# Rotary turn of the dilated heads: on a contiguous copy in token order, with even and odd tokens taken apart in the score products

## The chip, the cores and the metric

The kernel runs on one core of a Trainium2 chip, in float32 throughout. The metric is the device time of one execution in microseconds (us); lower is better. The engines are named as the profile names them: PE (TensorE products), PEld (its weight loads), DVE (VectorE), ACT (ScalarE), POOL (GpSimd), SP (SyncE, here a queue of loads).

## What is computed

Two layers of a decoder trunk for 256 tokens of width 1024. Each layer has a mixer (gated linear attention, retention, and a softmax attention over dilated windows, merged by gates), a layer norm, a SwiGLU block and a second norm. The change lies in the dilated attention, which has three groups of four heads of 128 channels:

```python
for g, (window, dilation) in enumerate(((128, 1), (512, 4), (2048, 16))):
    qg = _rotary(dq[:, :, g], pos, 32, 5e5)     # first 32 channels turned by the token's angle
    kg = _rotary(dk[:, :, g], pos, 32, 5e5)
    o_g, lse_g = _dilated_window_attention(qg, kg, dv[:, :, g], window, dilation)
```

With `x1` and `x2` the first and second 16 of the 32 channels, the turn is `x1*cos - x2*sin` and `x2*cos + x1*sin`. In groups 1 and 2 a query sees only keys whose distance is a multiple of 4 or 16, so even tokens meet only even ones and odd only odd ones.

## The kernel before

All weights pass through PE as units of 128 x 1024, loaded by SP. Each unit is split into two float32r parts: the high part is a copy on ACT (sometimes DVE), the low part a subtraction on DVE (`make_hi`, `make_lo`). A product with the weights is three products of parts. `a_pair` makes 256 channels (two heads) for all 256 tokens with 48 products of 256 columns into a PSUM tile of the pool `pm` (three tiles); `b_group` makes 512 channels for 128 tokens with 24 products of 512 columns.

The order of each engine's instructions is fixed when the program is built. A main stream emits the products with the weights; after each step `tick` gives every side generator one turn (softmax, norms, the turn of the heads), and then emits the splits of the next unit. A planner keeps a rough clock for each engine (`issue`); a side generator calls `settle` and is not resumed until the planner believes that its operands have been there for 2400 ns (`MARGIN`). The engines then run their own rows strictly in that order and wait for each other by semaphores.

For each dilated group the main stream makes the values (in groups 1 and 2 by even and odd tokens: `chunk(2)` takes every second token of the stationary operand), then q and k, two pairs of heads each. After each pair it starts `dil_rot` (line 473), which moves the pair from PSUM to a block of SBUF and turns the first 32 channels. With the last k pair it starts `dil_group` (line 491): score products (line 518), maxima on DVE (line 521), exponentials on ACT (line 527), transposes, products with v, and in groups 1 and 2 a trip of the result through DRAM (`scr`, lines 566 and 571) that brings the tokens back in order.

Before the change `dil_rot` works like this: a shuffle on DVE swaps the two halves of 32 channels from PSUM into a scratch block; ACT copies the pair into the block; for groups 1 and 2 this copy writes even tokens first, so that neighbouring tokens are written 128 elements apart. Then DVE multiplies the swapped channels by the sine table, multiplies the 32 channels, read from PSUM again, by the cosine table into the block, and adds the two. The PSUM tile is given back after the second multiplication. The ACT copy and the shuffle read the same PSUM tile, and the program lets the copy wait for the shuffle.

A line that is a helper's stands for many places: DVE, ACT and POOL instructions show line 118, products line 130, transposes line 134, most DMAs line 138. Of names in the rows, `pm` is a PSUM tile of the main stream, `px` one of side work, `f` a block of the shared SBUF pools, `r` a float32r block (split weights, among others), `xh` and `xl` the two parts of the layer's input, `cst` the constants (turning tables, masks).

Of the kernel before, what the change touches and what calls it, by code (L numbers as in the profile page):

```python
# [54 lines left out]
def trunk(ctx: ExitStack, tc: tile.TileContext, wst, xt_in, x_in, cst, tri, pcol, wga, wa2, lnp, out):  # L55
# [7 lines left out]

    # ---- a rough clock in ns for each engine and tile: side work goes to the tensor engine when its operands
    # should be there, so that the products with the weights needn't wait behind it ----
    clk = {"P": 0.0, "A": 0.0, "V": 0.0, "G": 0.0, "D": 0.0}
# [7 lines left out]
    def when(log, ap, e):  # L74
        """When the last access in this log to any of the columns is over, as seen by engine e."""
        name, a, b = span(ap)
        return max([t + (e != "P" and OWN if by == e else HOP) for x, y, t, by in log.get(name, ()) if x < b and a < y], default=0.0)
# [62 lines left out]
    def settle(*aps, margin=MARGIN):  # L140
        """For a side generator: go on when these tiles should be there."""
        while any(when(written, a, "P") + margin > clk["P"] for a in aps):
            yield

# [1 line left out]
    class Blocks:  # L146
# [3 lines left out]
        def get(self, n=1):  # L150
            """For a side generator: the next n free blocks."""
            while len(self.free) < n:
                yield
            return [self.free.pop(0) for _ in range(n)]

        def main(self, n=1):
            """For the main stream."""
            left = 3000
            while len(self.free) < n:
                tick()  # L160
                left -= 1
                assert left, "blocks"
            return [self.free.pop(0) for _ in range(n)]
# [9 lines left out]

# [1 line left out]
    state = {"dma": 0, "made": 0, "whole": 0, "calm": False, "touched": 0, "freed": 0, "cap": NR // 2}  # L175
# [3 lines left out]
    def halves(u):  # L179
        """The first unit goes by halves, for an early start."""  # L180
        return (slice(0, 512), slice(512, 1024)) if u == 0 else (slice(0, 1024),)
# [61 lines left out]

# [1 line left out]
    side = []  # L245

    def spawn(g):
        side.append(g)

    def tick():  # L250
        for g in list(side):
            try:
                next(g)
            except StopIteration:
                side.remove(g)
        # the next unit: its first part when the engine is free for it, the second when the first should be there
        need = state["touched"] + 2
# [24 lines left out]

# [1 line left out]
    XH = T([128, KT, S], "xh", 1, F32R)  # L284
    XL = T([128, KT, S], "xl", 1, F32R)
    xts = [F2.main()[0] for _ in range(4)]

    # the input comes in five pieces of k-tiles: 0, 1, 2-3, 4-5, 6-7
    PIECES = ((0, 1), (1, 2), (2, 4), (4, 6), (6, 8))
# [13 lines left out]

    # products of zeros while the first loads are under way bring the tensor engine to its full clock
    zero = F2.main()[0]
# [15 lines left out]
    PC = T([128, L, 32], "pcol")  # L321
    # the turning tables fill 32 partitions of their columns; the gate's second matrix and its bias lie beside them
    WA2 = C[32:49, COLS["dilc"][0]:COLS["dils"][1]].rearrange("p (l c) -> p l c", l=L)
# [8 lines left out]
    def start_rest():  # L332
        """What the first products don't need."""
        dma(nc.scalar, C[0:32, 0:512], cst[0:32, 0:512], 32)
# [47 lines left out]

# [1 line left out]
    def tokens(v, tt, dl):  # L384
        """128 tokens: the tt-th half, or with dl = 2 those of remainder tt by 2."""
        return v[:, tt * 128:tt * 128 + 128] if dl == 1 else v.rearrange("p (i c) -> p c i", c=2)[:, tt, :]
# [11 lines left out]
    def b_group(units, lh, ll, tt, ps, dl=1, last=False):  # L398
        """ps [128 tokens, 512] from units of [2 k-tiles, 512 columns], a step for each unit."""
        n = len(units)  # L400
        for i, u in enumerate(units):
            b_unit(u, i, n, lh, ll, tt, ps, dl)
            if last:
                free(u)
            if i < n - 1:
                tick()

    def a_pair(units, rh, rl, ps):
        """ps [128 columns, 2, 256 tokens] from units of [4 k-tiles, 256 columns]."""
        n = len(units)  # L410
# [21 lines left out]

# [1 line left out]
    def ln_first(tt, c, ps, st):  # L434
# [36 lines left out]

# [1 line left out]
    def dil_rot(g, ps, dst):  # L473
        """Two heads' channels [128, 2, 256 tokens] into dst, their first 32 turned; dilated groups have even tokens first."""
        dl = 2 if g else 1
        (blk,) = yield from F2.get()
        t = blk[0:32, :]
        src = ps.rearrange("p (h i c) -> p h i c", h=2, c=dl)
        V.stream_shuffle(t, ps[0:32, :], SWAP)
        d4 = dst.rearrange("p (h c i) -> p h i c", h=2, c=dl)  # L480
        tr, to = t.rearrange("p (h i c) -> p h i c", h=2, c=dl), d4[0:32]
        act(d4, src, AF.Copy)
        def table(name):
            return cs(name)[0:32].rearrange("p (i c) -> p i c", c=dl).unsqueeze(1).to_broadcast([32, 2, S // dl, dl])
        V.tensor_mul(tr, tr, table("dils"))
        V.tensor_mul(to, src[0:32], table("dilc"))
        PM.put(ps)
        V.tensor_add(to, to, tr)
        F2.put(blk)

    def dil_group(l, g, dblk, m, den, outs):
        """Scores, softmax numerators and their products with v; outs gets [128 tokens, 512] for each tile."""
        qb, kb = dblk[g, 0], dblk[g, 1]
# [13 lines left out]
        for tt in range(2):  # L507
            nb = tt + 1 if whole else 1
            n = 128 * nb
            k0 = 0 if whole else tt * 128  # L510
            b = yield from PS.get(nb)
# [4 lines left out]
            for h in range(H):  # L516
                o = b[h // per][:, (h % per) * n:(h % per) * n + n]
                mm(o, qT[:, h, tt * 128:tt * 128 + 128], kT[:, h, k0:k0 + n], start=True, stop=True)
            for h in range(H):
# [91 lines left out]

# [1 line left out]
    def gla_gates(l, E):  # L613
# [147 lines left out]

# [1 line left out]
    def ret_all(l, pss, vb, sg):  # L763
# [102 lines left out]
    def head_out(l, key, o, col):  # L866
        """A branch's [tokens, heads] transposed, times its norm's gain when col is given, and split."""
        OH, OL = OT[l, key] = yield from R.get(2)
# [22 lines left out]

# [1 line left out]
    for l in range(L):  # L893
# [3 lines left out]

        # the projections for the branches: a step by tokens has two tiles, one by channels two pairs of heads
        douts = {}
# [26 lines left out]

        # the first two have their units in turns: either tile of tokens, or piece of the first input, gives them work
        us = take(8)
# [26 lines left out]
        for g in range(3):  # L955
# [3 lines left out]
            for which in range(2):  # L959
                for hp in range(2):  # L960
                    us = take(2)
                    ps = PM.main()[0]
                    a_pair(us, xh, xl, ps)
                    if hp == 0:
                        dblk[g, which] = F4.main()[0]
                    spawn(dil_rot(g, ps, dblk[g, which][:, hp * 512:hp * 512 + 512]))
                    if which and hp:
                        spawn(dil_group(l, g, dblk, m, den, douts))
                    tick()
# [20 lines left out]

        # merge gates and branch projections, by pairs of 128 columns
        state["cap"] = (NR - 10) // 2
# [39 lines left out]

        # output projection, then the first norm
        state["cap"] = (NR - 4) // 2
# [16 lines left out]

        # SwiGLU: the first 512 channels by tokens, the others by channels
        state["cap"] = (NR - 5) // 2
# [91 lines left out]
        for tt in range(2):  # L1145
            # of the last tile, the first half of the columns ends before the second begins
            st = T([128, 2, 6], "lnst", 2)
# [60 lines left out]
def _sums(np):  # L1208
    """Within each chunk of 64, a sixteenth of the sum up to a token and of the sum after it."""
    i = np.arange(128)  # L1210
# [5 lines left out]
def _stream(np, w_in, w_branch, w_out, w_gate, w_up, w_down):  # L1216
    """All weights in the order of use, as units of [128, 1024]."""
    w = np.empty((L * UNITS, 128, 1024), np.float32)
# [100 lines left out]
```

## Time and profile before

| | |
|---|---|
| median of 3 runs | 1068.72 us (1066.67 to 1068.91) |
| profiled execution: span from first to last instruction | 1066.5 us |
| mean granted TensorE clock | 0.995 of full |
| PE busy | 1049.8 us (98%), 7122 products |
| DVE busy | 706.6 us (66%) |
| ACT busy | 491.8 us (46%) |
| DMA | 192.25 MB, mean 180 GB/s |

The profile's times are those of one execution. Its span leaves out what lies before the first and after the last instruction; no other time of that execution is given, and the median of the runs stands 2.2 us above its span. Products on PE overlap, and their ends are modelled, so PE's busy share says little about how densely they follow each other; the distance between starts says it.

### The profile page before, as it was taken

How to read it: one execution, taken by the hardware profiler on the slowest of the kernel's cores; microseconds unless marked ns; L12 is line 12 of the kernel's file. 1: busy time of each engine (PE TensorE's matmuls, PEld its weight loads, DVE VectorE, ACT ScalarE, POOL GpSimd, SP SyncE). 2: the span in 40 equal slices, each digit the busy share in tenths (PEclk: the TensorE clock that was granted, in tenths of full speed). 3: DMA queues.
4: the chain of work that ended last, by engine and by line, in shares of the span. 5: the costliest groups of instructions: out<-in, count | busy, mean ns of one | idle time of the engine just before them, and what ended most of it. 6: DMA issues, size and time to landing. Idle time of an engine off the chain costs nothing.

```text
span 1066.5 us, 17475 instructions
## 1 busy us (share of the span) xinstructions
PE 1049.8 (98%) x7122; PEld 956.9 (90%) x7122; DVE 706.6 (66%) x1065; ACT 491.8 (46%) x734; POOL 17.9 (2%) x24
## 2 busy tenths in 40 slices
PE   9999999999999999999999998999999999999997
PEld 7998977799998899999889998877999988999996
DVE  6798755767658756554688777476676686556454
ACT  6475554444445444343364554553443445444330
POOL 0000000000000000000000000000000000000000
PEclk9999999999999999999999999999999999999999
DMA  8786633426656574555376355343375666655521
GB/s 325 248 267 194 197 109 111 158 80 225 190 172 223 168 287 164 194 191 200 121 268 220 124 173 183 92 136 122 118 220 185 186 209 232 223 197 167 194 94 40
DMA packets 55667, 192.25 MB, mean 180 GB/s; under 512 B 6258, under 2 KB 7410, under 8 KB 55587
## 3 DMA queue, kind: packets, MB, share of 16 engines
q1 hardware_dynamic: 50400, 180.38, 51.4%
q10 hardware_dynamic: 5186, 10.76, 3.0%
q8 instruction: 56, 0.92, 0.3%
q14 instruction: 25, 0.20, 0.1%
HBM read 187.93 MB, written 3.18 MB: 179 GB/s over the span
## 4 chain that ended last, share of the span: by engine, by line
PE 90%; DVE 4%; DMA 3%; ACT 1%; issue 1%; SPq 0%; ACTq 0%; DVEq 0%
PE pm L130 70%; PE px L130 18%; DVE f L118 2%; PE px L134 2%; DMA scr<-f 2%; DVE r L118 2%; ACT f L118 1%; DMA stage<-in_wst_dram 0%; DMA f<-scr 0%; ACT r L118 0%; DVE xres L118 0%; SPq L138 0%; ACTq L138 0%; DVE lnst L118 0%; DVEq L1314 0%
## 5 line engine op out<-in xcount | busy, mean ns | idle before, releaser
L130 PE MATMUL pm<-xh,r 128*128 128x256 f32 x2688 | 478.2, 280 | 0.0
L118 DVE SCALAR_TENSOR_TENSOR r<-stage,r 128x1024 fp32r<-128x1024 f32 (+1 forms) x341 | 401.7, 1213 | 59.4 <-ACT r L118 57.1
L130 PEld LDWEIGHTS pm<-xh,r 128*128 128x128 f32 x2688 | 413.1, 189 | 1.1
L118 ACT ACTIVATE r<-stage 128x1024 fp32r<-128x1024 f32 (+1 forms) x328 | 332.8, 1051 | 91.8 <-issue 31.3
L130 PE MATMUL pm<-xl,r 128*128 128x256 f32 x1344 | 374.9, 279 | 0.0
L130 PEld LDWEIGHTS pm<-xl,r 128*128 128x128 f32 x1344 | 252.4, 188 | 0.9
L130 PE MATMUL pm<-r,xh 128*128 128x512 f32 x672 | 218.4, 406 | 0.8 <-ACT r L118 0.8
L130 PEld LDWEIGHTS pm<-r,xh 128*128 128x128 f32 x672 | 124.8, 192 | 29.3 <-issue 3.0
L130 PE MATMUL pm<-r,xl 128*128 128x512 f32 x336 | 133.6, 398 | 0.0
L118 ACT ACTIVATE f<-pm 128x512 f32<-128x512 f32 x72 | 50.8, 707 | 156.6 <-PE pm L130 106.1
L130 PE MATMUL px<-r,r 128*128 128x512 f32 x528 | 122.6, 389 | 0.0
L130 PEld LDWEIGHTS px<-r,r 128*128 128x128 f32 x528 | 97.9, 188 | 19.3
L130 PE MATMUL pm<-r,r 128*128 128x256 f32 (+1 forms) x768 | 115.1, 310 | 0.0
L130 PEld LDWEIGHTS pm<-r,r 128*128 128x128 f32 x768 | 105.2, 191 | 7.3
L118 DVE SCALAR_TENSOR_TENSOR f<-f,pm 128x512 f32<-128x512 f32 x52 | 35.6, 685 | 106.6 <-ACT f L118 89.9
L130 PEld LDWEIGHTS pm<-r,xl 128*128 128x128 f32 x336 | 64.6, 192 | 14.3
L130 PE MATMUL px<-f,f 128*128 128x128 f32 (+4 forms) x368 | 60.4, 304 | 6.3 <-DVE f L118 6.3
L130 PEld LDWEIGHTS px<-f,f 128*128 128x128 f32 (+2 forms) x368 | 48.7, 185 | 16.7 <-issue 8.5
L118 ACT ACTIVATE r<-f 128x512 fp32r<-128x512 f32 x28 | 17.7, 632 | 98.9 <-DVE f L118 98.9
L118 ACT ACTIVATE f<-pm,hcol 128x256 f32<-128x256 f32 x48 | 20.1, 471 | 58.1 <-PE pm L130 58.1
L118 ACT ACTIVATE f<-px 128x512 f32<-128x512 f32 (+2 forms) x52 | 25.0, 507 | 42.6 <-PE px L130 29.4
L118 DVE TENSOR_TENSOR f<-f,pm 128x512 f32<-128x512 f32 x22 | 15.1, 687 | 41.0 <-PE pm L130 40.8
(102 smaller groups left out, 498.6 us busy)
## 6 DMA issues: line engine op xcount, KB each, us to landing
stage<-in_wst_dram SPq DMA_DIRECT2D x339, 512.0 KB, 4.5
f<-in_lnp_dram ACTq DMA_DIRECT2D x8, 512.0 KB, 6.3
scr<-f ACTq DMA_DIRECT2D x8, 260.0 KB, 4.8
f<-scr ACTq DMA_DIRECT2D x4, 520.0 KB, 3.6
xres<-in_x_dram ACTq DMA_DIRECT2D x4, 256.0 KB, 4.0
out_dram<-xres SPq DMA_DIRECT2D x4, 256.0 KB, 2.0
f<-in_xt_dram SPq DMA_DIRECT2D x3, 256.0 KB, 9.1
cst<-in_cst_dram ACTq DMA_DIRECT2D x4, 192.0 KB, 3.8
```

What stands on the lines that cost most here:

```text
L118: return f(*a, **k)
L130: return nc.tensor.matmul(out, lhsT, rhs, **k)
L134: return nc.tensor.transpose(out, in_, ident)
```

## The change

`dil_rot` no longer knows the group. ACT first copies the pair from PSUM into the block in token order, and the PSUM tile is given back. DVE then does everything on SBUF: shuffle from the block into the scratch, sine on the scratch, cosine in place on the block, sum, all in token order. The score products of groups 1 and 2 take the even or the odd tokens by reading every second column of q (the stationary operand) and of k (the moving operand).

```diff
-    def dil_rot(g, ps, dst):
+    def dil_rot(ps, dst):
-        dl = 2 if g else 1
         (blk,) = yield from F2.get()
-        t = blk[0:32, :]
-        src = ps.rearrange("p (h i c) -> p h i c", h=2, c=dl)
-        V.stream_shuffle(t, ps[0:32, :], SWAP)
-        d4 = dst.rearrange("p (h c i) -> p h i c", h=2, c=dl)
-        tr, to = t.rearrange("p (h i c) -> p h i c", h=2, c=dl), d4[0:32]
-        act(d4, src, AF.Copy)
-        def table(name):
-            return cs(name)[0:32].rearrange("p (i c) -> p i c", c=dl).unsqueeze(1).to_broadcast([32, 2, S // dl, dl])
-        V.tensor_mul(tr, tr, table("dils"))
-        V.tensor_mul(to, src[0:32], table("dilc"))
+        act(dst, ps, AF.Copy)
         PM.put(ps)
-        V.tensor_add(to, to, tr)
+        t, o = blk[0:32, :], dst[0:32, :]
+        V.stream_shuffle(t, o, SWAP)
+
+        def times(x, name):
+            x2 = x.rearrange("p (h t) -> p h t", h=2)
+            V.tensor_mul(x2, x2, cs(name)[0:32].unsqueeze(1).to_broadcast([32, 2, S]))
+        times(t, "dils")
+        times(o, "dilc")
+        V.tensor_add(o, o, t)
         F2.put(blk)
...
-                mm(o, qT[:, h, tt * 128:tt * 128 + 128], kT[:, h, k0:k0 + n], start=True, stop=True)
+                if whole:
+                    mm(o, qT[:, h, tt * 128:tt * 128 + 128], kT[:, h, 0:n], start=True, stop=True)
+                else:
+                    mm(o, tokens(qT[:, h, :], tt, 2), tokens(kT[:, h, :], tt, 2), start=True, stop=True)
```

`tokens(v, tt, 2)` is the helper that the values already use: `v.rearrange("p (i c) -> p c i", c=2)[:, tt, :]`.

The planner sees other operands and so places side work differently. On PE, in layer 0, group 2: the score products (`px` from two `f` blocks, q and k) of the two tiles of tokens and the product with `gaT` of the gates' branch, between products with the weights for 128 tokens. Piece of the difference, before (-) and after (+):

```order
-L130 MATMUL px_112<-f_91,f_95 128x128 x4
 L130 MATMUL pm_106<-r_77,xh 128x512
 L130 MATMUL pm_106<-r_78,xh 128x512
 L130 MATMUL pm_106<-r_77,xl 128x512
 L130 MATMUL pm_106<-r_77,xh 128x512
 L130 MATMUL pm_106<-r_78,xh 128x512
 L130 MATMUL pm_106<-r_77,xl 128x512
-L130 MATMUL px_113<-f_91,f_95 128x128 x4
-L130 MATMUL px_109<-cst,gaT 128x256 x2
+L130 MATMUL px_112<-f_91,f_95 128x128 x4
+L130 MATMUL px_113<-cst,gaT 128x256 x2
```

The first tile's scores stand six products with the weights later, and the product with `gaT` comes ahead of the second tile's scores. In group 1, and in layer 1 as well, the scores move back by six such products in the same way.

On ACT, in layer 0, around the trip of group 1's result through DRAM (`scr`), while group 2's q is made (`f_95` is the block of group 2's q, `pm` the pair that is copied into it, `r` from `stage` the high part of a weight unit). Before:

```order
L118 ACTIVATE f_95<-pm_108 128x2x128x2
L118 ACTIVATE r_83<-stage 128x1024
L118 ACTIVATE f_92<-px_110 128x512
L138 DMA scr_145<-f_92 128x520
L118 ACTIVATE r_85<-stage 128x1024
L138 DMA f_92<-scr_145 128x2x520
L118 ACTIVATE f_95<-pm_106 128x2x128x2
L118 ACTIVATE r_87<-stage 128x1024
```

And now:

```order
L118 ACTIVATE f_95<-pm_108 128x512
L118 ACTIVATE r_83<-stage 128x1024
L118 ACTIVATE f_97<-px_109 128x512
L118 ACTIVATE r_85<-stage 128x1024
L118 ACTIVATE f_92<-px_110 128x512
L138 DMA scr_145<-f_92 128x520
L118 ACTIVATE f_95<-pm_106 128x512
L118 ACTIVATE r_87<-stage 128x1024
L138 DMA f_92<-scr_145 128x2x520
```

The copy of the second q pair (`f_95<-pm_106`) stood behind the read-back from `scr`; now it stands ahead of it. Layer 1 shows the same exchange.

On ACT, in layer 0, just behind group 2's scores (`f_102` and `f_104` are the two tiles' scores, `f_98` the log of the gates' branch, `f_95<-pm_106` a swish gate). Piece of the difference:

```order
 L118 ACTIVATE f_102,f_94<-f_102,nm 128x128 x4
-L118 ACTIVATE f_104,f_94<-f_104,nm 128x128 x4
 L630 ACT_TABLE_LOAD
-L118 ACTIVATE f_98<-px_109 128x512
+L118 ACTIVATE f_98<-px_113 128x512
 L118 ACTIVATE f_98<-f_98 128x512
 L118 ACTIVATE f_98<-f_98,one 128x512
+L118 ACTIVATE f_104,f_94<-f_104,nm 128x128 x4
 L118 ACT_TABLE_LOAD
 L118 ACTIVATE f_95<-pm_106 128x512
```

The second tile's exponentials now stand behind the log; on DVE the step that uses the log likewise stands ahead of the second tile's maxima.

## Rows read from the trace of the kernel before

**Rows 1.** The page, part 1: busy time of the engines.
```profile
PE 1049.8 (98%) x7122; PEld 956.9 (90%) x7122; DVE 706.6 (66%) x1065; ACT 491.8 (46%) x734; POOL 17.9 (2%) x24
```

**Rows 2.** Timeline of PE: start us, us, instruction, [idle before <- releaser]; score products.
```profile
99.38 0.68 PE L130 MATMUL px<-f,f 128*128 128x128 f32 x4 [0.84 <-DVE f L118]
...
131.69 0.63 PE L130 MATMUL pm<-r,xh 128*128 128x512 f32 x2
...
137.26 0.61 PE L130 MATMUL px<-f,f 128*128 128x128 f32 x4
140.12 0.80 PE L130 MATMUL px<-f,f 128*128 128x128 f32 x4 [2.25 <-DVE f L118]
...
665.76 0.79 PE L130 MATMUL px<-f,f 128*128 128x128 f32 x4 [3.17 <-DVE f L118]
```

**Rows 3.** Chain of work that ended last: start us, us, merged products.
```profile
111.25 0.89 PE px L130 x8
...
224.12 4.25 PE pm L130 x36
```

**Rows 4.** Stretches, core 0: us, busy of PE, PEld, DVE, ACT, POOL, granted PE clock, DMA.
```profile
140.60:144.00 3.40, 3.40 (x12) 2.82 (x12) 3.22 (x11) 1.25 (x7) 0.00 (x0) 0.51 0.35 94
...
665.70:670.00 4.30, 4.24 (x17) 3.70 (x18) 3.73 (x12) 1.60 (x8) 0.00 (x0) 0.60 0.38 110
```

**Rows 5.** Timeline of DVE ahead of group 2's scores, layer 0.
```profile
133.69 2.31 DVE L118 SCALAR_TENSOR_TENSOR r<-stage,r 128x1024 fp32r<-128x1024 f32 x2
...
135.95 0.72 DVE L118 STREAM_SHUFFLE f<-pm 32x512 f32<-32x512 f32 x1
136.70 0.68 DVE L118 TENSOR_TENSOR f<-f,cst 32x512 f32<-32x512 f32 x1
137.84 1.04 DVE L118 TENSOR_TENSOR f<-pm,cst 32x512 f32<-32x512 f32 x1 [0.45 <-ACT f L118]
138.91 1.05 DVE L118 TENSOR_TENSOR f<-f,f 32x512 f32<-32x512 f32 x1
```

**Rows 6.** Timeline of ACT: the last copy of layer 0; behind the read-back, layer 1.
```profile
136.70 1.10 ACT L118 ACTIVATE f<-pm 128x512 f32<-128x512 f32 x1 [3.34 <-DVE f L118]
...
649.84 1.11 ACT L118 ACTIVATE f<-pm 128x512 f32<-128x512 f32 x1 [3.39 <-DMA scr<-f]
```

**Rows 7.** Blocks f, 108 to 140 us (group 2): ns min/median/max, first and last start.
```profile
L118 DVE TENSOR_TENSOR f<-pm,cst x4: 1045/1098/1099, 115.7 to 137.8; 32x512 f32<-32x512 f32 x4
L118 DVE TENSOR_TENSOR f<-f,f x4: 1054/1109/1121, 116.8 to 138.9; 32x512 f32<-32x512 f32 x4
```

**Rows 8.** The same, 30 to 56 us (group 0, token order): DVE and ACT.
```profile
L118 DVE TENSOR_TENSOR f<-pm,cst x4: 678/679/679, 37.5 to 54.6; 32x512 f32<-32x512 f32 x4
...
L118 DVE TENSOR_TENSOR f<-f,f x4: 678/680/680, 38.3 to 55.3; 32x512 f32<-32x512 f32 x4
...
L118 ACT ACTIVATE f<-pm x5: 593/599/601, 29.8 to 53.9; 128x512 f32<-128x512 f32 x5
```

**Rows 9.** Timeline of PE: transposes of the dilated branch's result, both layers.
```profile
175.43 0.77 PE L134 MATMUL px<-cst,f 128*128 128x128 f32 x4 [0.27 <-DVE f L118]
...
701.35 0.77 PE L134 MATMUL px<-cst,f 128*128 128x128 f32 x4 [0.54 <-DVE f L118]
```

**Rows 10.** Weight loads into pm, ns: values by every second token; then tokens in order.
```profile
L130 PEld LDWEIGHTS pm<-r,xh x16: 194/194/198, 92.2 to 97.2; 128*128 128x128 f32 x16
...
L130 PEld LDWEIGHTS pm<-r,xh x4: 187/188/188, 131.6 to 132.4; 128*128 128x128 f32 x4
```

**Rows 11.** Timelines of DVE, ACT and PE behind group 2's scores, layer 0.
```profile
144.70 0.29 DVE L118 CUSTOM_DVE_ANT_0 f<-px,cst 128x128 f32<-128x128 f32 x1 [0.85 <-PE px L130]
...
147.54 1.28 ACT L630 ACT_TABLE_LOAD   x1
...
154.00 0.68 DVE L118 SCALAR_TENSOR_TENSOR r<-f,r 128x512 fp32r<-128x512 f32 x1
...
156.65 0.72 PE L130 MATMUL px<-r,tri 128*128 128x256 f32 x4
```

More of the change, by code (lines that the diff above doesn't have):

```diff
@@ L509, in dil_group @@
             n = 128 * nb
-            k0 = 0 if whole else tt * 128
             b = yield from PS.get(nb)
@@ L965, in trunk @@
                         dblk[g, which] = F4.main()[0]
-                    spawn(dil_rot(g, ps, dblk[g, which][:, hp * 512:hp * 512 + 512]))
+                    spawn(dil_rot(ps, dblk[g, which][:, hp * 512:hp * 512 + 512]))
                     if which and hp:
```

## The prediction

> **What bounds the kernel now.** I read the page's busy times first: PE is busy 98% of the span, DVE 66%, ACT 46% [rows 1]. So time can only be won where PE stands still or runs slowly, and a faster DVE or ACT is worth nothing elsewhere. Next the timeline of PE, looking for starts that lie too far apart. Four passes of a score product take 0.45 us, from eight in 0.89 us [rows 3]. But the first two heads of group 2 start at 137.26 and the other two at 140.12, 2.41 us late, of which the profile shows 2.25 us as idle and waiting for DVE; the same happens at 665.76 in layer 1 (3.17 us idle), and on a smaller scale in layer 0, group 1, at 99.38 (0.84 us) [rows 2]. The reader is to see that the second pair of heads is late, not the first: it is the last turn, that of the last k pair, that PE waits for. These three are all of this kind.
>
> Why it is late, the timelines of DVE and ACT show. The turn is a relay: shuffle on DVE (135.95), copy on ACT (starts 136.70, after 3.34 us of idling for DVE), cosine on DVE (137.84, after 0.45 us of idling for ACT), sum (138.91 to 139.96) [rows 5, 6]. One turn thus holds DVE for 4.0 us, and two low parts of weights lie between turns, 2.3 us [rows 5]. Together that is 6.3 us per pair of heads, while PE needs 48 products at 4.25/36 = 0.118 us, 5.7 us [rows 3]. So DVE loses some 0.6 us per pair and is late by several us at the last one. Layer 1 adds a block: ACT stands 3.39 us behind the read-back from DRAM before it may copy [rows 6].
>
> [...]
>
> **The change, part by part.**
>
> *DVE work of the turn.* In groups 1 and 2 the cosine multiplication takes 1.10 us and the sum 1.11 us [rows 7]; group 0, which already is in token order, shows 0.68 us for both [rows 8]. That is 0.85 us less for each of 16 turns, 13.6 us of DVE. On its own it is worth nothing (DVE isn't the bound); it counts through the last turn. The shuffle's source moves from PSUM to SBUF, and so does the cosine's. The rows have no shuffle from SBUF; the multiplications from PSUM and from SBUF take the same 0.68 us [rows 8], so I leave it at 0.72. Were it to take 0.3 us more or less, the slack below would hide it.
>
> *The relay.* The copy now waits for PE alone and takes 0.60 us instead of 1.10 [rows 6, 8]; then DVE does its four steps in a row, 0.72 + 3 x 0.68 plus gaps, 2.9 us. The added wait is that of the shuffle for the copy. Behind it on DVE stand low parts of weights; they were late by more before, since DVE idled for ACT in the middle of the turn. With 2.9 + 2.3 = 5.2 us per pair against 5.7 on PE, DVE no longer falls behind; it can lose at most the 0.9 us until the copy is done, and only when it has nothing older to do.
>
> *The read-back.* ACT's copy of the second q pair stands ahead of it now. The block of 3.4 us falls into the 5.7 us in which PE makes the next pair, so no copy is late by it.
>
> *The scores' place on PE.* They move back by six products of 512 columns, some 0.23 us each (137.26 - 131.69 = 5.57 us cover 24 products of 256 columns, 2.8 us, and 12 of 512), 1.4 us. So they stand 7.0 us behind the end of the last pair; the turn is done 0.3 + 0.6 + 2.9 = 3.8 us behind it. Slack 3.2 us: all three gaps should go.
>
> *The sum.* Gaps: 0.84, 2.25 and 3.17 us of idling [rows 2], and 0.16 us more each, as the starts at 137.26 and 140.12 show (2.86 apart, less 0.45 for four passes, is 2.41): together 6.7. Slow clock: (1 - 0.51) x 3.4 + (1 - 0.60) x 4.3 = 1.7 + 1.7 = 3.4 us [rows 4]. Further on, the transposes of the branch's result wait 0.27 and 0.54 us for DVE [rows 9], 0.8 together; these now stand behind six more products, and I count them as gone. That is 10.9 us.
>
> *Strided operands of the scores.* 32 products, each four-pass product seen as two records, 64 records at 0.11 us, 7.1 us in all. On the stationary side the trace has the same step: the values' loads by every second token take 194 ns against 188 [rows 10], in the shadow of products of 512 columns. A moving operand with a step isn't in the trace. From below the cost is nothing (a gain is excluded: the columns are as many). From above, DVE's own price for uneven access, 1.10 to 0.68, would be 0.62 x 7.1 = 4.4 us. But DVE's slow operand jumped 128 elements between neighbours and went back, and here the step is two. The nearest row is that of the loads on the same engine; I take 0.
>
> [...]
>
> *The log behind the scores.* The second tile's exponentials now stand behind the table load and the log on ACT, and DVE's step with the log ahead of the second tile's maxima. Here DVE and ACT work in turns and whatever goes ahead delays the rest. The cumulative sums of the gates need what the log leads to: it was ready at 154.7 and taken at 156.65, a slack of 2.0 us [rows 11]. The second tile's maxima and exponentials, from 144.70 to 147.54, 2.8 us [rows 11], stood ahead of the log and still stand ahead of the swish gate and the split that end this chain, but DVE's and ACT's steps no longer overlap around the log, which costs up to these 2.8 us. So between 0 and 0.8 us is lost in each layer; the low parts that DVE did in between are out of the way, so I take 0.15 each, 0.3.
>
> Together 10.9 - 0.3 = 10.6 us. From the profiled span of 1066.5 us that gives 1055.9; the median of the runs lies 2.2 above that span, so **1058.1 us**.
>
> **The rivals.**
>
> *A, strided scores cost as DVE's did:* +4.4 us, 1062.5. For it: no row has such a moving operand. Against: rows 10.
>
> *B, a new wait takes the gap's place:* the cumulative sums stand still for 1.5 us in both layers, and the clock drops as in rows 4, 1.7 us each time: 2 x 3.2 = 6.4 us given back, 1064.5. For it: a slack of 2.0 us against a shift of up to 2.8. Against: 1.5 us is nearly twice the 0.8 that this leaves, so another delay must come on top.
>
> *C, the last turn is still late:* the shuffle now waits for ACT, and if ACT has older work in front of each copy, the turn ends as late as before; the gaps then close by the 1.4 us of the moved scores at most, and with the clock still dropping some 4 us or less are won: 1065, or 1068 if the copies are later still. For it: ACT is named 0.45 us a turn today. Against: ACT's rows ahead of the copies are two splits, and ACT idled 3.3 us at these very places [rows 6].
>
> *D, slower:* PE reads every second column at a quarter of the rate, in all 64 records: 3 x 7.1 = 21 us lost, 10.6 won, 1079. It decides as soon as a pass takes more than 2.5 times its 0.11 us; below that the change still gains. Against: weight loads with the same step cost 3% more, not four times [rows 10].
>
> *E, nothing changes:* the gaps go, but the new order of the side work makes others of the kind of rows 9, 0.3 to 0.5 us each. It would take some twenty of them to eat 8.5 us or more: 1066.6 to 1070.8. Against: the trace of before has two.
>
> **How the numbers follow.** A measurement of this kernel can tell 0.2%, 2.1 us, from no change. Forecast 0.64, with 1055.5 to 1060 of its own (the lowest run lies 2.05 us under the median, and the log's term may be 1.3 us more); A 0.08; B 0.11; C 0.08, half of it within 0.2%; D 0.04; E 0.05. From these: faster 0.64 + 0.08 + 0.11 + 0.04 = 0.87; the same 0.04 + 0.05 = 0.09; slower 0.04. The range is 1055.0 to 1064.5: it takes in the forecast with its bounds, A and B, and leaves out C, D and E.
>
> **What would show it.** Right: no idling for DVE on PE at the scores of groups 1 and 2; granted clock 1.00 there; PE's busy time almost unchanged while the span falls; DVE's multiplications and sums at 0.68 us throughout and its busy time some 13 us lower; ACT's copies at 0.60 us, ended by PE and not by DVE; eight score passes still in about 0.9 us. Wrong: score passes further apart than 0.11 us (A, D); a wait of PE for DVE or ACT at the cumulative sums (B), at the scores again (C), or no wait and the same span (E).

## The result, and the profile after

The changed kernel takes 1056.32 us (median; 1055.49 to 1057.61), beside 1068.82 for the kernel before on the same chip: ratio 0.9886 [0.9872, 0.99]: faster by 1.1%, clear of the scatter. Measured again later, it took 1057.36 beside 1066.78, ratio 0.990 [0.9881, 0.992]. The profiled span fell from 1066.5 to 1054.1 us. One execution of b_g2late and one of step8, two of the experiments below, took over three times as long as all others and are left out of their medians.

The profile's page of the changed kernel: busy us (share of the span) of each engine, which answers to [rows 1]; then the engines' shares of the chain that ended last.

```profile
PE 1044.4 (99%) x7122; PEld 953.9 (90%) x7122; DVE 695.3 (66%) x1066; ACT 485.5 (46%) x733; POOL 17.9 (2%) x24
...
PE 99%; DMA 0%; DVE 0%; SPq 0%; issue 0%; DVEq 0%; ACT 0%
```

PE is busy 5.4 us less with as many products; the stretches of [rows 4] at a granted clock of 0.51 and 0.60 account for 3.4 us of this, estimated from their clock and length; the rest I can't assign. DVE's busy time fell by 11.3 us.

The timeline of PE (start us, us, instruction, idle before in brackets where there is any), the scores and what stands around them:

```profile
98.84 1.10 PE L130 MATMUL px<-f,f 128*128 128x128 f32 x8
99.69 0.72 PE L130 MATMUL pm<-r,xh 128*128 128x512 f32 x2
...
129.87 0.63 PE L130 MATMUL pm<-r,xh 128*128 128x512 f32 x2
...
136.81 1.10 PE L130 MATMUL px<-f,f 128*128 128x128 f32 x8
...
657.11 1.10 PE L130 MATMUL px<-f,f 128*128 128x128 f32 x8
```

Where [rows 2] show two rows of x4 with 0.84, 2.25 and 3.17 us of idling between them, there is one row of x8 without a bracket: both pairs of heads go through at once. The granted clock stays up. These are the stretches of group 2's scores, columns as in [rows 4]:

```profile
136.00:142.00 6.00, 6.00 (x34) 4.97 (x33) 2.17 (x10) 2.86 (x9) 0.00 (x0) 1.00 0.55 176
...
656.00:663.00 7.00, 7.00 (x38) 5.79 (x37) 3.03 (x11) 3.54 (x10) 0.00 (x0) 1.00 0.47 152
```

The clock is 1.00, where it was 0.51 and 0.60. The turn itself is as the diff lets one expect. The timelines of DVE and ACT, group 2's last k pair in layer 0:

```profile
131.08 0.72 DVE L118 STREAM_SHUFFLE f<-f 32x512 f32<-32x512 f32 x1
131.84 1.28 DVE L118 TENSOR_TENSOR f<-f,cst 32x512 f32<-32x512 f32 x2
133.16 0.68 DVE L118 TENSOR_TENSOR f<-f,f 32x512 f32<-32x512 f32 x1
```

```profile
119.77 0.60 ACT L118 ACTIVATE f<-pm 128x512 f32<-128x512 f32 x1 [0.41 <-ACT f L118]
...
124.05 0.38 ACTq L138 DMA_DIRECT2D f<-scr  x1
...
130.07 0.60 ACT L118 ACTIVATE f<-pm 128x512 f32<-128x512 f32 x1 [0.47 <-PE pm L130]
```

The last pair ends at 129.87, the turn at 133.84, 3.97 us behind it, and the scores start 6.94 us behind it. That leaves a slack of 2.97 us.

### The profile page after: what moved, and what is told of

It is laid out like the page before. It is cut to its first block, busy times and chain, and to the rows that moved or that the text cites. A ratio compares the mean times of both kernels' runs of the same rounds, so it can differ in the third digit from the quotient of the medians.

```text
span 1054.1 us, 17500 instructions
## 1 busy us (share of the span) xinstructions
PE 1044.4 (99%) x7122; PEld 953.9 (90%) x7122; DVE 695.3 (66%) x1066; ACT 485.5 (46%) x733; POOL 17.9 (2%) x24
## 4 chain that ended last, share of the span: by engine, by line
PE 99%; DMA 0%; DVE 0%; SPq 0%; issue 0%; DVEq 0%; ACT 0%
PE pm L130 77%; PE px L130 19%; PE px L134 2%; DMA stage<-in_wst_dram 0%; DVE xres L118 0%; SPq L138 0%; DVE lnst L118 0%; DVE r L118 0%; DVEq L1314 0%; ACT r L118 0%; DVE mv L118 0%; DVE ve L118 0%
## 5 line engine op out<-in xcount | busy, mean ns | idle before, releaser
L130 PE MATMUL pm<-r,xh 128*128 128x512 f32 x672 | 215.2, 401 | 0.8 <-ACT r L118 0.6
L118 ACT ACTIVATE f<-pm 128x512 f32<-128x512 f32 x72 | 42.6, 593 | 131.3 <-PE pm L130 129.4
```

What stands on the lines that cost most here:

```text
L118: return f(*a, **k)
L130: return nc.tensor.matmul(out, lhsT, rhs, **k)
```

## The experiments

Three theories for the gain. **Theory 1** (mine): the quick turn lets DVE keep up, and the last turn is done in time. **Theory 2**: the turn hardly matters; the scores stand six products (1.4 us) further back, and that is enough. **Theory 3**: DVE's lesser work as such. **Theory 4** came up after the first runs and stands in the later expectations: what counts is the read-back from DRAM, whose place on ACT moves with that of the scores, and the place itself; the turn's speed only helps. All ratios are to the kernel before, measured on the same chip; the name of a run is that of its expectation.

**The old turn with the scores moved back (b_mid, b_late).** The kernel before, with a larger margin, so that the planner puts the scores later: six products in b_mid, where the change has them, and more in b_late.

```diff
-        yield from settle(qb, kb)
+        yield from settle(qb, kb, margin=MARGIN + 1400)
```

(+ 2800 in b_late.)

> The kernel before with its old turn; only the planner's margin ahead of the scores is 1400 ns larger, so that the scores of groups 1 and 2 stand exactly where the changed kernel has them, six products (1.4 us) later. Theory 1 (PE lost the gaps at the last turn, and the clock behind them): each gap shrinks by 1.4 us, 1.00 to 0, 2.41 to 1.0, 3.33 to 1.9; 1065.0 if the clock still falls behind the two that are left, 1061.6 if it does not. Theory 2 (the new place of the scores does it all): 1056.3, as the changed kernel. Theory 3 (the time is DVE work that went away, wherever it stood): 1068.8, no change.

> The kernel before with its old turn; the margin ahead of the scores is 2800 ns larger, the first scores of group 2 stand 12 products (2.8 us) later than before, those of group 1 18 (4.2 us). Theory 1: gaps 0, 0 and 0.5 us, clock full, 1057 to 1058.5, with DVE's busy time as before (706 us). Theory 2: something else than 1056.3 only by the place itself; it makes no forecast below 1058. Theory 3: 1068.8.

Measured: b_mid 1055.78 us, ratio 0.9874 [0.9846, 0.9903]; b_late 1056.71, 0.9876 [0.9843, 0.9908]. The old turn with the larger margin wins all that the change wins; theory 1 had b_mid at 1061.6 to 1065.0. Later the two went side by side on one chip:

> The changed kernel, unaltered, beside the next two on one chip. 1056.3, and 0.988 of the kernel before.

> The kernel before with the old turn and the scores six products later, unaltered, beside the changed kernel on the same chip. If the quick turn's 11 us of DVE work and its strided scores are worth nothing at the end: within 0.1% of the changed kernel. If the quick turn gains something besides: 1 us or more above it.

The change 1057.36, the old turn with the larger margin 1057.15 (ratio 0.9902 [0.9883, 0.992]): no difference. Theory 3 falls with it, since DVE in b_mid does no less work than before. The page of b_mid, part 1:

```profile
PE 1044.3 (99%) x7122; PEld 953.4 (90%) x7122; DVE 708.0 (67%) x1066; ACT 492.7 (47%) x733; POOL 17.9 (2%) x24
```

By my account b_mid should have kept gaps, since the old turn ended 8.27 us behind the last pair (131.69 to 139.96, [rows 2, 5]) and the scores now stand 7 us behind it. The timelines of b_mid's PE, DVE and ACT show why not:

```profile
130.05 0.63 PE L130 MATMUL pm<-r,xh 128*128 128x512 f32 x2
...
137.00 1.05 PE L130 MATMUL px<-f,f 128*128 128x128 f32 x8
```

```profile
131.76 0.72 DVE L118 STREAM_SHUFFLE f<-pm 32x512 f32<-32x512 f32 x1
132.52 0.68 DVE L118 TENSOR_TENSOR f<-f,cst 32x512 f32<-32x512 f32 x1
133.65 1.10 DVE L118 TENSOR_TENSOR f<-pm,cst 32x512 f32<-32x512 f32 x1 [0.45 <-ACT f L118]
134.79 1.09 DVE L118 TENSOR_TENSOR f<-f,f 32x512 f32<-32x512 f32 x1
```

```profile
119.95 1.11 ACT L118 ACTIVATE f<-pm 128x512 f32<-128x512 f32 x1 [0.41 <-ACT f L118]
...
124.23 0.38 ACTq L138 DMA_DIRECT2D f<-scr  x1
```

Same steps, same lengths, same wait of 0.45 us as in [rows 5]; yet the turn ends at 135.88, 5.83 us behind the pair instead of 8.27. The whole row of turns runs 2.4 us earlier, and ACT shows where that comes from: the copy of the second q pair goes at 119.95, ahead of the read-back from DRAM (124.23); b_late has the same order (119.58 and 125.02). In the kernel before it is the other way round, on ACT's timeline:

```profile
123.72 0.38 ACTq L138 DMA_DIRECT2D f<-scr  x1
124.15 1.11 ACT L118 ACTIVATE f<-pm 128x512 f32<-128x512 f32 x1 [2.91 <-DMA scr<-f]
```

The issue of the read-back stands still on ACT until the write to DRAM has landed, and the copy behind it stands still with it, 2.91 us. DVE waits for this copy within the turn. Its cosine and sum in that turn, on DVE's timeline, first before, then b_mid:

```profile
125.30 1.10 DVE L118 TENSOR_TENSOR f<-pm,cst 32x512 f32<-32x512 f32 x1 [3.25 <-ACT f L118]
126.43 1.12 DVE L118 TENSOR_TENSOR f<-f,f 32x512 f32<-32x512 f32 x1
```

```profile
121.09 1.11 DVE L118 TENSOR_TENSOR f<-pm,cst 32x512 f32<-32x512 f32 x1 [1.04 <-ACT f L118]
122.23 1.12 DVE L118 TENSOR_TENSOR f<-f,f 32x512 f32<-32x512 f32 x1
```

The wait is 2.2 us longer in the kernel before. From this sum to that of the last turn, two turns later, 12.5 us pass in the kernel before and 12.6 in b_mid, while PE makes a pair in 5.7 us: DVE makes up nothing, and the delay is still there at the last turn. The same margin, in group 1, had moved group 1's scores, and with them the trip through DRAM, behind that copy. So the change holds three things that need to be told apart: the turn, the place of group 2's scores, and the read-back's order.

**Parts of the turn (relay_only, contig_only).** The first keeps the even-first layout, but ACT copies first and DVE works on SBUF; on DVE the sine now goes over the jumps, and the sum no longer does. The second has token order and strided scores, but DVE still shuffles from PSUM and ACT copies after it.

```diff
+        act(d4, ps.rearrange("p (h i c) -> p h i c", h=2, c=dl), AF.Copy)
+        PM.put(ps)
...
-        V.stream_shuffle(t, ps[0:32, :], SWAP)
...
-        act(d4, src, AF.Copy)
+        V.stream_shuffle(t, dst[0:32, :], SWAP)
...
```

```diff
+        V.stream_shuffle(t, ps[0:32, :], SWAP)
         act(dst, ps, AF.Copy)
...
+        times(o, ps[0:32, :], "dilc")
         PM.put(ps)
...
-        V.stream_shuffle(t, o, SWAP)
```

(The first is against before, the second against the change; dots stand for lines left out. In the second the cosine's operand too comes from PSUM.)

> ACT copies first and DVE does everything behind it on SBUF, as in the changed kernel, but with even tokens first, so that the copy, the sine and the cosine still go over jumps of 128 elements (1.10 us each) and the scores read packed operands; DVE's work per turn is as before within 0.1 us. Theory 1: DVE needs 3.7 + 2.3 = 6.0 us per pair against 5.7, but no longer stands for ACT; the last turn ends some 5.1 to 6.5 us behind the last pair, the scores stand 7.0 behind it: no gap, clock full, 1056 to 1058. Theory 3: 1068.8, since DVE's work did not shrink.

> Token order and strided scores as in the changed kernel, but the old relay: shuffle and cosine read PSUM, ACT copies behind the shuffle. Group 2's scores stand at their old place (5.6 us behind the last pair), and the read-back from DRAM stands ahead of the second q pair's copy in layer 1 as before. Theory 1: 2.9 + 2.3 = 5.2 us of DVE per pair, so it is not late in layer 0: no gap there; in layer 1 the block of ACT is made up by 0.5 us per pair and 0 to 0.8 us of gap are left; 1056.5 to 1059. Theory 2: the gaps of group 2 stay with their clock, 1066 to 1068. Theory 3: 1056.3.

Measured: relay_only 1056.88, ratio 0.9879 [0.9854, 0.9904]; contig_only 1058.49, 0.9893 [0.9867, 0.9919]. In both the read-back has fallen behind the copy, in both layers; contig_only's expectation had it ahead of the copy in layer 1, so this run doesn't try its turn with the old order. In contig_only group 2's scores are where they were before (5.57 us behind the pair), and no gap is left at them; what stays are the waits of [rows 9], on PE's timeline:

```profile
169.31 0.77 PE L134 MATMUL px<-cst,f 128*128 128x128 f32 x4 [0.30 <-DVE f L118]
...
691.24 0.77 PE L134 MATMUL px<-cst,f 128*128 128x128 f32 x4 [0.58 <-DVE f L118]
```

Together 0.88 us of its 1.6 to 2.7 us over the runs above; they are gone in the change, b_mid and relay_only, where group 2's scores stand later. The rest is no more than the runs scatter.

**The quick turn alone, and the two places alone (a_early, b_g1late, b_g2late).** a_early is the change with a margin smaller by 1400 ns: group 1's and group 2's scores are back at their old places, and in layer 1 the read-back too. The other two are the kernel before with the larger margin in one group only: group 1 (its scores, and the read-back with them), or group 2 (its scores alone). One line of each, in this order:

```diff
+        yield from settle(qb, kb, margin=MARGIN - 1400)
+        yield from settle(qb, kb, margin=MARGIN + (1400 if g == 1 else 0))
+        yield from settle(qb, kb, margin=MARGIN + (1400 if g == 2 else 0))
```

> The changed kernel with a margin ahead of the scores that is 1400 ns smaller: the scores of groups 1 and 2 stand at their places of before, and in layer 1 the read-back from DRAM again stands ahead of the second q pair's copy; in layer 0 it stays behind. What is left of the change is the quick turn. Theory 1 (the quick turn is enough): no gap in layer 0, where the turn ends 3.9 us behind the last pair and the scores stand 5.6 behind it; 1056.3 to 1058. Theory 4 (the place of the scores and that of the read-back did it, the turn's speed only helps): in layer 1 the blocked copy leaves DVE about 1.1 us late at the scores, 1058.6 without and 1060.3 with a fall of the clock, transposes waiting 1.2 us as in the run with the old relay included.

> The kernel before, old turn; only group 1's scores stand six products later, group 2's where they were. By that the read-back stands behind the second q pair's copy in both layers. Theory 4: DVE is then not held by the read-back, the last turn ends 5.8 us behind the last pair as in the run with the moved scores, and the second pair of heads is wanted at 6.0: gap 0 to 0.2 us; with 1.2 us of waits at the transposes 1057.5 to 1058.5. Theory 2 (the place of group 2's scores alone): group 2's gaps stay, 1067.9.

> The kernel before, old turn; only group 2's scores stand six products later; the read-back stays ahead of the copy in both layers. Theory 4: the last turn is as late as before, the gaps shrink by 1.4 us to 1.0 and 1.9, group 1's 1.0 stays; 1066.1 if the clock falls behind them, 1062.7 if not. Theory 2: 1057.3.

Measured: a_early 1058.69, ratio 0.9909 [0.9886, 0.9932]; b_g1late 1058.31, 0.991 [0.9891, 0.9929]; b_g2late 1063.06, 0.9953 [0.9935, 0.9971]. The timeline of PE in a_early, b_g1late and b_g2late, in that order:

```profile
656.96 0.63 PE L130 MATMUL px<-f,f 128*128 128x128 f32 x4
658.17 0.71 PE L130 MATMUL px<-f,f 128*128 128x128 f32 x4 [0.58 <-DVE f L118]
```

```profile
657.09 0.61 PE L130 MATMUL px<-f,f 128*128 128x128 f32 x4
657.91 0.68 PE L130 MATMUL px<-f,f 128*128 128x128 f32 x4 [0.21 <-DVE f L118]
```

```profile
98.31 0.68 PE L130 MATMUL px<-f,f 128*128 128x128 f32 x4 [0.89 <-DVE f L118]
...
138.94 0.68 PE L130 MATMUL px<-f,f 128*128 128x128 f32 x4 [0.76 <-DVE f L118]
...
153.63 0.38 PE L130 MATMUL px<-r,tri 128*128 128x256 f32 x1 [0.38 <-ACT r L118]
154.44 0.62 PE L130 MATMUL px<-r,tri 128*128 128x256 f32 x3 [0.42 <-DVE r L118]
...
662.09 0.68 PE L130 MATMUL px<-f,f 128*128 128x128 f32 x4 [1.62 <-DVE f L118]
```

The order on ACT in layer 0, first b_g1late (copy, then read-back), then b_g2late (read-back, then copy):

```profile
120.75 1.10 ACT L118 ACTIVATE f<-pm 128x512 f32<-128x512 f32 x1 [0.41 <-ACT f L118]
...
125.17 0.40 ACTq L138 DMA_DIRECT2D f<-scr  x1
```

```profile
122.49 0.38 ACTq L138 DMA_DIRECT2D f<-scr  x1
122.92 1.11 ACT L118 ACTIVATE f<-pm 128x512 f32<-128x512 f32 x1 [2.74 <-DMA scr<-f]
```

With the quick turn at the old places, layer 0 (where the read-back stays behind the copy) has no gap at the scores. In layer 1, where the read-back stands ahead of the copy again (644.27, the copy at 644.69 after 3.26 us of idling), 0.58 of the 3.17 us is left; theory 4 had expected 1.1. With the old turn and the old place of group 2's scores, but the read-back moved (b_g1late), group 2's gap is gone in layer 0 and 0.21 us is left in layer 1. With the old turn and the read-back ahead (b_g2late), the later place takes 1.5 to 1.6 us off each group 2 gap and no more; 1063.06 lies between theory 4's 1062.7 and 1066.1, as the clock fell behind one of the two gaps (0.50) and not behind the other (1.00). So theory 2 falls as a whole. At group 2's scores the quick turn is nearly enough, and the read-back's order is nearly enough; the place of the scores is not.

Group 1's gap in layer 0 (0.84 us, [rows 2]) is another matter: the read-back comes after it. It closes with the quick turn at the old place (a_early) and with the old turn at the later place (b_g1late), and stays in b_g2late. No run moved the read-back without group 1's scores under the old turn.

b_g2late also brings what rival B described, cumulative sums that wait for ACT and DVE (0.38 and 0.42 us), in layer 0; relay_only has such a wait in layer 1 (0.42 us).

**The strided operands (halves, step8).** The change, but group 1's and 2's scores read packed halves of the tokens (other tokens, as many columns), or every eighth column of both operands (one line of each, in this order). In both, the scores of groups 1 and 2 are those of other pairs of tokens than the reference's.

```diff
+  mm(o, qT[:, h, tt * 128:tt * 128 + 128], kT[:, h, tt * 128:tt * 128 + 128], start=True, stop=True)
+  q8 = qb[:, 0:1024].rearrange("p (i c) -> p c i", c=8)[:, 2 * h + tt, :]
```

(k8 likewise.)

> The changed kernel, but the scores of groups 1 and 2 read the first or second half of the tokens, packed, in place of the even or odd ones, so the result is not the reference's; everything else stays. It prices the step of two: 64 passes at 0.106 us in the changed kernel against 0.101 with packed operands would be 0.3 us, less than the runs can tell; eight passes in 0.81 us from start to start in place of 0.85.

> [...] If a step costs nothing on PE in float32: 1056.3, eight passes in 0.89 us. If uneven access costs what it costs DVE, 1.6 times: 1060.7, eight passes in 1.44 us. [...]

Measured: halves 1056.82, ratio 0.9897 [0.9878, 0.9915], beside 1057.36 for the change on the same chip; step8 1064.57, 0.9971 [0.9959, 0.9983]. Eight passes and the product behind them, on PE's timeline, first halves, then step8 (group 1, layer 0):

```profile
100.88 1.06 PE L130 MATMUL px<-f,f 128*128 128x128 f32 x8
101.69 0.72 PE L130 MATMUL pm<-r,xh 128*128 128x512 f32 x2
```

```profile
103.70 2.06 PE L130 MATMUL px<-f,f 128*128 128x128 f32 x8
105.41 0.82 PE L130 MATMUL pm<-r,xh 128*128 128x512 f32 x2
```

From start to start eight passes take 0.81 us packed, 0.85 by every second column (98.84 to 99.69 in the change) and 1.71 by every eighth. 64 passes at 0.005 us more are 0.3 us for the change, under what a run can tell; at 0.107 us more they are 6.9 for step8. Not measured side by side with the change: 1064.57 less 1057.36 or 1056.32, 7.2 to 8.3 us. A clock that fell to 0.50 adds to the 6.9. Windows of step8 behind group 2's scores of layer 1, columns as in [rows 4]:

```profile
664.20:667.80 3.60, 3.60 (x15) 2.91 (x15) 1.36 (x10) 0.33 (x2) 0.00 (x0) 1.00 0.78 257
667.80:671.20 3.40, 3.40 (x13) 2.99 (x11) 0.00 (x0) 3.34 (x11) 0.00 (x0) 0.50 0.09 36
```

By the starts on PE's timeline that costs 0.8 us: the six products of 512 columns behind the product with `gaT` take 2.29 us (667.24 to 669.53), 1.49 in the change (138.90 to 140.39). The eight passes behind them take 1.72 us (669.53 to 671.25), as long as those of group 1 above. 6.9 and 0.8 are 7.7. So what rivals A and D feared exists at a step of eight, at twice the time a pass (0.214 us against 0.106), but not at a step of two.

## Why the prediction was right, and where its reason was not

**The time.** 1058.1 was forecast, 1056.32 and 1057.36 measured; as a gain, 10.6 us against 12.5 and 9.4. The median still lies 2.2 us above the profiled span; 1.9 of this separate the profiled execution's own time (1055.96) from its span.

**Gaps, slow clock, transposes.** Right as terms of the sum. The three gaps are gone (6.7 us), the clock stays at 1.00 there (3.4), the transposes of [rows 9] no longer wait (by starts 0.43 and 0.70 us, 1.1 instead of 0.8). The rest of the 12.4 us of span, some 1 us, I can't assign. Two profiles of the changed kernel differ by as much (1054.1 and 1055.5), and there a cause is seen: in the second (after_again) PE waits 1.27 us for ACT at its start, and the clock then stands at 0.50 for 3.3 us, long before the dilated heads. The timeline of PE and a window, columns as in [rows 4]:

```profile
7.29 0.51 PE L130 MATMUL pm<-r,xh 128*128 128x512 f32 x1 [1.27 <-ACT r L118]
```

```profile
8.40:11.70 3.30, 3.30 (x9) 2.62 (x8) 1.92 (x2) 2.03 (x3) 0.00 (x0) 0.50 1.02 404
```

The profiled execution of the first waits 0.61 us there and keeps the clock (1.00 from 4 to 12 us).

**The turn's length and the scores' place.** Right: 3.97 us behind the last pair instead of 3.8, scores 6.94 behind it instead of 7.0, eight passes in 0.85 us, copies of 0.60 us, none of which waits for DVE. The trace shows a product of the scores as two records, 0.106 us apart, and these are the passes counted here; that one product has four, as the prediction says, no run shows. DVE saved 11.3 us instead of 13.6; 1.3 of the difference is one more high part that DVE makes now (14 instead of 13).

**The log.** Mis-sized, 0.3 us counted and nothing lost. The timelines of DVE and PE of the changed kernel, which answer to [rows 11]:

```profile
150.10 0.68 DVE L118 SCALAR_TENSOR_TENSOR r<-f,r 128x512 fp32r<-128x512 f32 x1
```

```profile
151.40 0.63 PE L130 MATMUL px<-r,tri 128*128 128x256 f32 x4
```

Ready at 150.78, taken at 151.40: of the 2.0 us of slack 0.6 is left, and PE doesn't wait, nor in layer 1. Rival B was near.

**Why the gaps close.** Here the reasoning failed. I wrote that DVE "loses some 0.6 us per pair and is late by several us at the last one", named the block of the read-back for layer 1 only, and saw in it only a block that the next copy would not feel. The pace was right: the turns follow each other at 6.3 us. But layer 0 has the block too (2.91 us), and 2.2 of the 8.27 us by which the last turn ended behind its pair were inherited from it, since DVE, slower than PE, had no time to make them good. Without the block the old, slow turn leaves no group 2 gap in layer 0 and 0.21 us in layer 1 (b_g1late); the lost pace alone does not make these gaps. The step that failed is "The read-back": I priced its new place at nothing and did not ask what its old place had cost at the end of the row of turns.

The change has the quick turn, the moved read-back and the later scores, and the pairs of two that were tried left no gap (quick turn and moved read-back: a_early's layer 0; moved read-back and later scores: b_mid). So the number came out right, in part by luck: the new order of ACT, which I counted at nothing, would have closed nearly all of group 2's gaps by itself. The quick turn with later scores and the read-back at its old place wasn't tried. Against the kernel before on the same chip, the quick turn with the read-back moved in one layer is worth 8.9 us (a_early), group 1's later scores with the read-back moved 9.3 (b_g1late; 1.0 of it is group 1's own gap), group 2's place 4.5 (b_g2late), all of them together 9.4 to 12.5. These overlap and don't add.

## What to carry to other kernels

When a consumer waits for the last of a row of equal steps, look for the block at the first of them as well as for the pace: a delay ahead of the row reaches its end undiminished if the row has no time to spare (here 2.2 us, with turns 6.3 us apart behind pairs of 5.7). A waiting DMA issue in a computing engine's stream is such a block (here 2.91 and 3.39 us on ACT), and where it stands may be a side effect of another number (here a planner's margin). Before rewriting the work that is late, try the number that places it and its consumer: here a larger margin over both groups was worth as much as the rewrite (1057.15 us beside 1057.36), mostly because it moved the waiting DMA issue (b_g1late) and less because the consumer came later (b_g2late). So look in the trace at what else such a number has moved.

## What the runs showed of the hardware

A float32 product of 128x128 costs 5% more with both operands at a step of two (0.106 us a pass against 0.101) and twice as much at a step of eight (0.214). For ACT's copy the step of 128 elements in the written block costs 1.10 us against 0.60 packed.

The clock fell to 0.50 in step8 without a gap: PE shows 3.60 us busy of 3.60 ahead of it, but with score passes at twice their usual distance (0.214 us). It did so once: behind the same scores in layer 0 it stayed at 1.00. And not every gap makes it fall: in b_g2late 0.76 us of idling was followed by a stretch at 1.00, 1.62 us by one at 0.50 (its windows, columns as in [rows 4]):

```profile
138.50:142.00 3.50, 3.06 (x14) 2.35 (x15) 3.44 (x9) 0.00 (x0) 0.00 (x0) 1.00 0.13 19
...
664.70:668.10 3.40, 3.40 (x14) 3.01 (x13) 1.09 (x10) 2.22 (x9) 0.00 (x0) 0.50 0.84 276
```

The waits of PE at the start of the profiled executions, for ACT, narrow this. Waits of 1.00 us (b_late) and 1.03 (halves) left the clock at 1.00; 1.27 (after_again), 1.39 (b_mid_again) and 1.91 us (b_g1late) were followed by 3.3 us at 0.50 to 0.51. So in these cases the granted clock stayed at 1.00 behind a wait of up to 1.03 us and fell behind one of 1.27 us or more.
